# Moving S5 and the convolution within a mixer, and regrouping three products of RWKV

## The chip, the cores and the metric

One NeuronCore of one Trainium2 chip runs the whole kernel in one launch. The metric is the device time in microseconds; three runs of the kernel before gave 1250.41, 1250.13 and 1246.07 us, so the median is 1250.13. The engines are TensorE (PE, with its weight loads as PEld), VectorE (DVE), ScalarE (ACT), GpSimd (POOL) and SyncE (SP, which issues most transfers).

## The reference, cut to what matters

The program is a trunk of two layers on 256 positions of width 1024, float32. Each layer adds half a SwiGLU, then a mixer, then half a second SwiGLU; a last norm ends it. The mixer projects the normalised input and lets four branches work on it side by side:

```
for l in range(DEPTH):
    x = x + 0.5 * swiglu(rmsnorm(x, ffn1_norm[l]), ...)
    h = rmsnorm(x, mix_norm[l]);  p = h @ w_in[l]
    u_a, u_b, r_p, k_p, v_p, z_in, b_g, c_g, gate_pre = split(p)
    y_a = s5_mixer(u_a, ...)                # diagonal complex state space, 16 groups
    y_b = pool_mixer(u_b, ...)              # trailing means
    y_c = rwkv7_mixer(h, r_p, k_p, v_p, ...)  # delta rule, decay per channel, 4 heads
    y_d = b_g * causal_conv3(c_g * z_in)    # short convolution
    merged = sum over the four of (y_b @ w_branch[l, b]) * sigmoid(gate_b)
    x = x + merged @ w_out[l]
    x = x + 0.5 * swiglu(rmsnorm(x, ffn2_norm[l]), ...)
```

RWKV's recurrence is computed in chunks of 64 positions: for every chunk and head a matrix of pairs is formed (the products of keys, gates and receptances with their decays), a triangular matrix of it is inverted, and the states are carried from chunk to chunk.

## The kernel before, in words

**Weights.** All large products go through units: a unit is a 256x512 block of a weight matrix. SyncE loads it (raw), ScalarE rounds it to the high part (wh, L253), VectorE forms the residue (wl = raw - wh, L225 through `finish`), and TensorE takes three matmuls for each 128 rows: high by high (L259), high by low weight (L260), low by high (L261). Four units have room at a time. The high part of a unit is issued six steps before its first matmul, its residue five steps before.

**Order of the work.** The order on every engine is fixed at build time by the class `Flow`. The main thread is a list of steps; in a mixer one step is two ticks, and a tick is three matmuls of 512 columns. The branches are generator threads that yield waits: `wA(n)` means "go on at the start of the n-th next step", `wT(n)` "after n ticks", and `wM(n, b)` "after n ticks, when b PSUM banks are free, and only one such thread in a tick", the first in the list (RWKV, convolution, S5, pool). These numbers decide only where instructions stand in the queue of their engine; at run time every engine works through its queue in order, and an instruction waits for its inputs alone.

**The steps of a mixer**, counted from 0 at the low-rank columns: 0 to 39 the projections (low-rank; r and k; ua and ub; v and z; bg and cg), 40 to 55 the gates of the pool branch, 56 to 59 that branch's product (Y[1]), 60 to 75 the gates of the convolution branch, 76 to 79 its product, then S5's (96 to 99) and RWKV's.

**RWKV (L909 to L1325).** At steps 36 to 40 VectorE forms the decays, bvec and kp, rk (L1033), the planes of W and BK; GpSimd forms DG (L1030, the diagonal with a chunk's last decay), copies the values v into two planes of W (L1053), and forms the two halves of KB (L1054, L1055, keys times the decay to the chunk's end). At ticks 90 and 94 follow the pair matrices Gm (matmuls L1073), which read BK and three planes of W. GpSimd then takes small diagonal blocks of them (dg, L1084, sixteen copies), forms the levels Bl and Rd, and four rounds of inversion run from tick 116 on (L1102): each is a matmul on Bl and Tm, a copy Xm on ScalarE, a matmul on Rd and Xm, and Tm = p + Tm on VectorE, three ticks apart. The values in W and KB are first read by the transposes L1123 and L1124 (tick 100), DG by MT (L1236).

**S5 (L1328 to L1436).** us goes to memory and comes back as U8 (L1342). `wM(38, 1)` (L1344) counts from there to the matmuls sT; from sT follow, in fixed distances, sN, the transposes sS, the copies sX, six VectorE operations (gA, gB, gt), two scans (L1378), two GpSimd products, Hs (L1385), the matmuls sY (L1392), the gelu and the glu product. The steps are such that sT stands at tick 98.

**Convolution (L1480 to L1508).** zc = cg * zin at step 44; `wA(14)` (L1496) puts the taps (cv, L1499 and L1501) at steps 58 and 59, the product with bg at 60 and the split into high and low at 61.

Of the kernel before, what the change touches and what calls it, by code (L numbers as in the profile page):

```python
# [11 lines left out]
AF = mybir.ActivationFunctionType  # L12
# [12 lines left out]
C = 64  # L25
# [25 lines left out]
def wA(n=1):  # L51

    return ("A", n, 0)
# [17 lines left out]
def wM(n=1, banks=0):  # L71

    return ("M", n, banks)
# [98 lines left out]
def trunk_kernel(ctx: ExitStack, tc: tile.TileContext, a, out, dbg=None):  # L172
    nc = tc.nc
    ve, sc, gp, pe = nc.vector, nc.scalar, nc.gpsimd, nc.tensor
# [19 lines left out]
    def cc(name):  # L194
        o, n = CONST_COLS[name]
        return cst[:, o:o + n]
# [11 lines left out]
    def bank(name="pb"):  # L208
        assert fl.banks > 0
        fl.banks -= 1  # L210
        return pp.tile([128, 512], F32, name=name, tag="pb")

    def free(n=1):
        fl.banks += n
        assert fl.banks <= NB
# [8 lines left out]
    def tt(o, i0, i1, op=ALU.mult, eng=ve):  # L224
        eng.tensor_tensor(out=o, in0=i0, in1=i1, op=op)  # L225
# [292 lines left out]
    def col(l, name, i=0):  # L518
        r, n = vrow[name]
        return vec[:, r + l * n + i:r + l * n + i + 1]  # L520
# [277 lines left out]
    def mixer(l):  # L798
# [3 lines left out]
        def et(shape, nm, dt=F32):  # L802
            return st["mp"].tile(shape, dt, name=nm, tag="e", bufs=NE)

        def ft(shape, nm):
            return st["mp"].tile(shape, F32, name=nm, tag="f", bufs=NF)

        def e2(nm):
            return et([128, 2, S], nm)

        def enter():
            st["mp"] = es_.enter_context(tc.tile_pool(name=f"mix{l}", bufs=1))
            spawn(rwkv())
            spawn(conv())
            spawn(s5())
            spawn(pool())
# [76 lines left out]
        def until(name):  # L893
            while name not in got:
                yield wA(1)
# [3 lines left out]
        def ysplit(b, src):  # L899
            h, lo = et([128, 2, S], f"yh{b}", F32R), et([128, 2, S], f"yl{b}", F32R)  # L900
            split(h, lo, src)
            Y[b] = (h, lo)

        def dump(nm, src):
            if dbg is not None and l == 0:
                sp.dma_start(out=dbg[nm].rearrange("(j p) t -> p j t", p=128), in_=src)


        def rwkv():  # L909
# [9 lines left out]
            def tshift(ps, i, nm):  # L919
                z = e2(nm)  # L920
                for j in range(2):
                    sc.activation(z[:, j], ps[:, j], AF.Copy, scale=om[:, 2 * i + j:2 * i + j + 1])
                for j in range(2):
                    ve.scalar_tensor_tensor(out=z[:, j, 1:], in0=ps[:, j, :S - 1],
                                            scalar=col(l, "rwkv_mu_rkv", 2 * i + j),
                                            in1=z[:, j, 1:], op0=ALU.mult, op1=ALU.add)
                return z
# [76 lines left out]
            v_ = tshift(got["v"], 2, "v")  # L1004
# [16 lines left out]
            Pt, Pm, iP, PC = L0[:, 0], L0[:, 1], L1[:, 0], L1[:, 1]  # L1021
            bvec, kp = e2("bvec"), e2("kp")
# [4 lines left out]
            yield wA(1)  # L1027
            DG = et([128, 8, C], "DG")
            id8 = cc("id64").unsqueeze(1).to_broadcast([128, 8, C])
            tt(DG, id8, Pt[:, :, C - 1:C].to_broadcast([128, 8, C]), eng=gp)  # L1030
            rk = e2("rk")
            for j in range(2):
                ve.scalar_tensor_tensor(out=rk[:, j], in0=r_[:, j], scalar=col(l, "rwkv_r_k", j), in1=kp[:, j],  # L1033
# [3 lines left out]
            W = st["mp"].tile([128, 4, 6, C], F32, name="W")  # L1037
            KB2 = ft([128, 4, 4, C], "KB2")
            BK = ft([128, 4, 4, C], "BK")

            def me(t_):
                return t_.rearrange("p j (m e t) -> p (j m) e t", m=2, e=2)

            def mf(t_):
                return t_.rearrange("p (q e) t -> p q e t", e=2)
# [4 lines left out]
            tt(W[:, :, 2::3], me(r_), mf(Pt))  # L1050
            yield wA(1)
            tt(BK[:, :, 1:3], me(kp), mf(iP))
            gp.tensor_copy(W[:, :, 1::2][:, :, 0:2], me(v_))  # L1053
            tt(KB2[:, :, 0::3], me(bvec), mf(PC), eng=gp)  # L1054
            tt(KB2[:, :, 1:3], me(kp), mf(PC), eng=gp)  # L1055

            def small_tile(nm):
                return st["mp"].tile([128, 8, 32], F32, name=nm, tag="q", bufs=7)
# [5 lines left out]
            for j in range(2):  # L1064
                yield wM(10 if j == 0 else 4, 2)
                ps = [bank("gm").rearrange("p (c t) -> p c t", c=4) for _ in range(2)]
                for c in range(4):
                    m, o = c // 2, c % 2
                    for e in range(2):
                        es = slice(64 * e, 64 * e + 64)  # L1070
                        lhs = BK[es, 2 * j + m, 2 * o:2 * o + 2].rearrange("p k t -> p (k t)")
                        rhs = W[es, 2 * j + m, 0:3:2] if o == 0 else W[es, 2 * j + m, 4:6]
                        pe.matmul(ps[e][:, c], lhsT=lhs, rhs=rhs, start=True, stop=True)  # L1073
                yield wA(1)
                for e in range(2):
                    h = 2 * j + e
                    g_ = et([128, 4, 128], f"Gm{h}")
                    tt(g_, ps[e], maskb)
                    free()
                    Gm.append(g_)  # L1080
                    gv = g_.rearrange("p (m o) s -> p o m s", o=2)
                    for q in range(4):
                        qs, cs = slice(32 * q, 32 * q + 32), slice(32 * (q % 2), 32 * (q % 2) + 32)
                        gp.tensor_copy(dg[qs, 2 * h:2 * h + 2], gv[qs, q // 2, :, cs])  # L1084
# [157 lines left out]
            for c in range(3):  # L1242
                for h in range(4):
                    j, e = h // 2, h % 2
# [14 lines left out]
            for c in range(1, 3):  # L1259
                yield wM(2 if c > 1 else 4, 1)  # L1260
                p = bank("zc").rearrange("p (j s) -> p j s", s=C)
                for h in range(4):
                    j, e = h // 2, h % 2
# [64 lines left out]
        def s5():  # L1328
# [12 lines left out]
            U8 = et([128, G, 32], "U8")  # L1341
            sp.dma_start(out=U8, in_=ud.rearrange("g h i b -> (h i) g b"))  # L1342

            yield wM(38, 1)  # L1344
            sT = bank("sT").rearrange("p (u s) -> p u s", u=4)
            for u in range(4):
                for q in range(4):
# [132 lines left out]
        def conv():  # L1480
            yield from until("z_in")
            yield wA(1)
            zin = e2("zin")
            sc.activation(zin, got["z_in"], AF.Copy)
            free()
            yield from until("bg")
            yield wA(1)
            bg = e2("bg")
            sc.activation(bg, got["bg"], AF.Copy)
            free()  # L1490
            yield from until("cg")
            yield wA(1)
            zc = e2("zc")
            tt(zc, got["cg"], zin)
            free()
            yield wA(14)  # L1496
            cv = e2("cv")
            for j in range(2):
                sc.activation(cv[:, j], zc[:, j], AF.Copy, scale=col(l, "conv_w", 4 + j))  # L1499
                for w in (1, 0):  # L1500
                    ve.scalar_tensor_tensor(out=cv[:, j, 2 - w:], in0=zc[:, j, :S - 2 + w],  # L1501
                                            scalar=col(l, "conv_w", 2 * w + j), in1=cv[:, j, 2 - w:],
                                            op0=ALU.mult, op1=ALU.add)
                yield wA(1)
            tt(cv, cv, bg)
            yield wA(1)
            ysplit(3, cv)
            dump("yd", cv)  # L1508
# [185 lines left out]
```

## Time and profile before

| | |
|---|---|
| median of three runs | 1250.13 us (1246.07 to 1250.41) |
| profiled execution | 1247.8 us, span 1246.0 us |
| mean granted TensorE clock | 0.997 |
| TensorE busy | 1224.4 us, 98% |
| VectorE, ScalarE, GpSimd busy | 761.9, 616.8, 372.8 us |

Busy shares are means over the whole span. The mixers lie at about 208 to 410 us and 822 to 1024 us; the other stretches are the feed-forward halves. A wait of an engine is listed with what ended it; where the time of an instruction includes waiting for a shared resource, the instruction shows as longer.

### The profile page before, as it was taken

What the parts mean: (1) busy time and instruction counts of PE and PEld (TensorE: products, weight loads), DVE (VectorE), ACT (ScalarE), POOL (GpSimd) and SP (SyncE); (2) the same over time, 40 slices, a digit from 0 to 9 for tenths busy, and PEclk for the clock granted to TensorE, in tenths of its full rate; (3) what the DMA queues carried; (4) which work ended last, traced back from release to release, by engine and by line L of the source; (5) the groups of instructions that cost most, each with busy time, mean ns of one, the idle gap of its engine ahead of it and who ended that gap; (6) DMA issues with size and microseconds to landing.
All of it is one profiled execution on the core that took longest, in us unless ns stands there. A gap on an engine that the chain in (4) does not pass through costs nothing.

```text
span 1246.0 us, 18893 instructions
## 1 busy us (share of the span) xinstructions
PE 1224.4 (98%) x7280; PEld 1000.1 (80%) x7280; DVE 761.9 (61%) x943; ACT 616.8 (50%) x787; POOL 372.8 (30%) x504
## 2 busy tenths in 40 slices
PE   8999999999999999999999999999999999999997
PEld 6888878887778888888888887888777788888885
DVE  6955656488566665554465555474885667555543
ACT  6454435665444464444364444366654445544433
POOL 4694394054132000000069454313512220000001
PEclk9999999999999999999999999999999999999999
DMA  8676555554446566655676565566443556666561
GB/s 255 182 220 182 182 177 165 179 148 139 123 133 196 176 185 186 186 181 191 187 200 179 177 193 179 158 189 181 152 122 105 158 187 193 188 186 186 185 191 63
DMA packets 139922, 216.28 MB, mean 174 GB/s; under 512 B 30348, under 2 KB 42488, under 8 KB 139832
## 3 DMA queue, kind: packets, MB, share of 16 engines
q1 hardware_dynamic: 138552, 213.63, 56.8%
q10 hardware_dynamic: 1120, 1.40, 0.3%
q8 instruction: 57, 0.93, 0.3%
q0 software_dynamic: 160, 0.05, 0.1%
q14 instruction: 33, 0.27, 0.1%
HBM read 212.29 MB, written 1.57 MB: 172 GB/s over the span
## 4 chain that ended last, share of the span: by engine, by line
PE 93%; DVE 5%; issue 1%; ACT 0%; DMA 0%; POOLq 0%; SPq 0%; POOL 0%; DVEq 0%; ACTq 0%
PE acc L259 29%; PE acc L260 28%; PE acc L261 28%; PE pb L271 3%; DVE wl L225 1%; PE inv L1102 1%; DVE cv L1501 0%; PE pb L778 0%; DVE rk L1033 0%; PE gm L1073 0%; DMA vr<-in_ffn_norm_dram 0%; PE lr L953 0%; PE wu L1207 0%; PE sY L1392 0%; DVE mg L225 0%
## 5 line engine op out<-in xcount | busy, mean ns | idle before, releaser
L225 DVE TENSOR_TENSOR wl<-raw,wh 128x1024 fp32r<-128x1024 f32 (+1 forms) x398 | 506.7, 1274 | 293.9 <-ACT wh L253 287.8
L253 ACT ACTIVATE wh<-raw 128x1024 fp32r<-128x1024 f32 (+1 forms) x393 | 415.0, 1056 | 416.9 <-PE acc L261 399.4
L259 PE MATMUL acc<-wh,xh 128*128 128x512 f32 x1152 | 462.0, 401 | 0.0
L260 PE MATMUL acc<-wl,xh 128*128 128x512 f32 x1152 | 450.2, 391 | 1.0 <-DVE wl L225 0.8
L261 PE MATMUL acc<-wh,xl 128*128 128x512 f32 x1152 | 450.3, 391 | 0.0
L259 PEld LDWEIGHTS acc<-wh,xh 128*128 128x128 f32 x1152 | 216.9, 188 | 47.7 <-issue 4.5
L261 PEld LDWEIGHTS acc<-wh,xl 128*128 128x128 f32 x1152 | 216.8, 188 | 46.4
L260 PEld LDWEIGHTS acc<-wl,xh 128*128 128x128 f32 x1152 | 217.1, 188 | 44.6 <-DVE wl L225 2.3
L259 PE MATMUL acc<-wh,hh 128*128 128x512 f32 x352 | 139.4, 396 | 0.0
L261 PE MATMUL acc<-wh,hl 128*128 128x512 f32 x352 | 137.6, 391 | 0.0
L260 PE MATMUL acc<-wl,hh 128*128 128x512 f32 x352 | 137.3, 390 | 0.0
L225 POOL TENSOR_TENSOR wl<-raw,wh 128x1024 fp32r<-128x1024 f32 x3 | 7.2, 2385 | 255.8 <-ACT wh L253 255.8
L261 PEld LDWEIGHTS acc<-wh,hl 128*128 128x128 f32 x352 | 66.1, 188 | 15.3
L259 PEld LDWEIGHTS acc<-wh,hh 128*128 128x128 f32 x352 | 66.1, 188 | 14.9 <-issue 1.3
L260 PEld LDWEIGHTS acc<-wl,hh 128*128 128x128 f32 x352 | 66.1, 188 | 13.9
L431 DVE SCALAR_TENSOR_TENSOR hd<-acc,rs,sg 128x512 f32<-128x512 f32 (+1 forms) x48 | 33.7, 703 | 33.3 <-PE acc L261 29.9
L336 POOL TENSOR_SCALAR pre<-ss 128x1 f32<-128x1 f32 x2 | 0.4, 224 | 171.4 <-ACT junk L284 171.4
L225 POOL TENSOR_TENSOR mg<-mg,gate 128x512 f32<-128x512 f32 x16 | 29.6, 1867 | 67.2 <-DVE gate L225 67.2
L222 DVE TENSOR_TENSOR hl<-pb,hh 128x512 fp32r<-128x512 f32 (+1 forms) x48 | 28.8, 642 | 32.3 <-ACT hh L221 32.2
L221 ACT ACTIVATE hh<-pb 128x512 fp32r<-128x512 f32 (+1 forms) x48 | 24.4, 561 | 42.2 <-PE pb L271 42.2
L424 ACT ACTIVATE sg<-acc,rs 128x512 f32<-128x512 f32 (+1 forms) x48 | 31.1, 654 | 20.6 <-PE acc L261 18.8
L794 POOL COPY LK<-LKt 128x512 f32<-128x512 f32 x8 | 11.0, 1403 | 66.1 <-DMA LKt<-kp 66.1
(349 smaller groups left out, 1149.0 us busy)
## 6 DMA issues: line engine op xcount, KB each, us to landing
raw<-in_w_in_dram SPq DMA_DIRECT2D x96, 512.0 KB
raw<-in_ffn_w_down_dram SPq DMA_DIRECT2D x88, 512.0 KB
raw<-in_ffn_w_up_dram SPq DMA_DIRECT2D x80, 512.0 KB
raw<-in_ffn_w_gate_dram SPq DMA_DIRECT2D x79, 512.0 KB
raw<-in_w_branch_dram SPq DMA_DIRECT2D x16, 512.0 KB
raw<-in_w_out_dram SPq DMA_DIRECT2D x16, 512.0 KB
raw<-in_ffn_w_gate_dram SPq DMA_DIRECT2D x18, 256.0 KB
raw<-in_ffn_w_up_dram SPq DMA_DIRECT2D x16, 256.0 KB
```

The costliest lines, as they stand in the source:

```text
L221: sc.activation(dh, src, AF.Copy)
L222: eng.tensor_tensor(out=dl, in0=src, in1=dh.bitcast(F32), op=ALU.subtract)
L225: eng.tensor_tensor(out=o, in0=i0, in1=i1, op=op)
L253: sc.activation(self.h, self.r, AF.Copy)
L259: pe.matmul(ps, lhsT=lh, rhs=wh, start=first, stop=False)
L260: pe.matmul(ps, lhsT=lh, rhs=wl, start=False, stop=False)
L261: pe.matmul(ps, lhsT=ll, rhs=wh, start=False, stop=last)
L271: pe.transpose(b[:, j * 128:(j + 1) * 128], src[:, j * 128:(j + 1) * 128], ident)
L424: sc.activation(sg[:, :n], pg[:, :n], AF.Silu, scale=rstd[t])
L431: ve.scalar_tensor_tensor(out=hd[:, :n], in0=pu, scalar=rstd[t], in1=sg[:, :n], op0=ALU.mult, op1=ALU.mult)
L794: gp.tensor_copy(LK[:, 4 * (q - 1 + h_):4 * (q + h_)], LKt[:, 4 * h_:4 * h_ + 4].rearrange("p g i h -> p g h i"))
L1102: pe.matmul(p[qs, u], lhsT=lhs[qs, u], rhs=rhs[qs, u], start=True, stop=True)
```

## The change

1. DG (L1030) is formed behind the second pair matrices, in the loop over j, instead of before rk.
2. Both halves of KB (L1054, L1055) are formed behind the first pair matrices.
3. The values are copied into W by ScalarE instead of GpSimd (L1053).
4. S5's sT comes 28 ticks behind the load of U8 instead of 38 (L1344).
5. The taps of the convolution come 22 steps behind zc instead of 14 (L1496).

All matmuls, transfers and operands stay as they are.

```
             DG = et([128, 8, C], "DG")
             id8 = cc("id64").unsqueeze(1).to_broadcast([128, 8, C])
-            tt(DG, id8, Pt[:, :, C - 1:C].to_broadcast([128, 8, C]), eng=gp)
             rk = e2("rk")
...
             tt(BK[:, :, 1:3], me(kp), mf(iP))
-            gp.tensor_copy(W[:, :, 1::2][:, :, 0:2], me(v_))
-            tt(KB2[:, :, 0::3], me(bvec), mf(PC), eng=gp)
-            tt(KB2[:, :, 1:3], me(kp), mf(PC), eng=gp)
+            sc.activation(W[:, :, 1::2][:, :, 0:2], me(v_), AF.Copy)
...
                         pe.matmul(ps[e][:, c], lhsT=lhs, rhs=rhs, start=True, stop=True)
                 yield wA(1)
+                if j == 0:
+                    tt(KB2[:, :, 0::3], me(bvec), mf(PC), eng=gp)
+                    tt(KB2[:, :, 1:3], me(kp), mf(PC), eng=gp)
+                else:
+                    tt(DG, id8, Pt[:, :, C - 1:C].to_broadcast([128, 8, C]), eng=gp)
                 for e in range(2):
...
-            yield wM(38, 1)
+            yield wM(28, 1)
             sT = bank("sT").rearrange("p (u s) -> p u s", u=4)
...
-            yield wA(14)
+            yield wA(22)
             cv = e2("cv")
```

## Rows read from the trace of the kernel before

**Rows 1.** The page: busy us by engine, and the chain that ended last.
```profile
PE 1224.4 (98%) x7280; PEld 1000.1 (80%) x7280; DVE 761.9 (61%) x943; ACT 616.8 (50%) x787; POOL 372.8 (30%) x504
...
PE 93%; DVE 5%; issue 1%; ACT 0%; DMA 0%; POOLq 0%; SPq 0%; POOL 0%; DVEq 0%; ACTq 0%
```
**Rows 2.** Waits of TensorE, whole span: us in total, times, longest.
```profile
PE inv L1102 <- DVE Tm L225: 5.0, 2, 2.5
PE inv L1102 <- issue: 1.0, 1, 1.0
PE acc L260 <- DVE wl L225: 0.8, 2, 0.4
PE inv L1102 <- DVE Tm L1137: 0.5, 2, 0.2
```
**Rows 3.** Timeline of TensorE, layer 0: start, us, instruction [idle before].
```profile
284.70 1.08 PE L1349 MATMUL sT<-LS,U 128*32 128x128 f32 x32
...
306.54 0.40 PE L259 MATMUL acc<-wh,xh 128*128 128x512 f32 x1
...
307.24 0.39 PE L259 MATMUL acc<-wh,xh 128*128 128x512 f32 x1
...
310.58 0.82 PE L1102 MATMUL inv<-Tm,Bl 32*32 32x32 f32 x64 [2.50 <-DVE Tm L225]
...
312.82 0.40 PE L259 MATMUL acc<-wh,xh 128*128 128x512 f32 x1
```
**Rows 4.** Timeline of TensorE, layer 1.
```profile
924.06 1.08 PE L1102 MATMUL inv<-Tm,Bl 32*32 32x32 f32 x64 [2.50 <-DVE Tm L225]
...
927.63 0.39 PE L259 MATMUL acc<-wh,xh 128*128 128x512 f32 x1
```
**Rows 5.** Stretch of layer 1: us; busy PE, PEld, DVE, ACT, POOL; clock; DMA share, GB/s.
```profile
926.00:927.00 1.00, 1.00 (x4) 0.72 (x3) 1.00 (x2) 0.00 (x0) 0.00 (x0) 0.50 0.65 250
```
**Rows 6.** Timeline of VectorE, layer 0, RWKV's products.
```profile
266.87 2.08 DVE L225 TENSOR_TENSOR wl<-raw,wh 128x1024 fp32r<-128x1024 f32 x1
268.88 2.27 DVE L1033 SCALAR_TENSOR_TENSOR rk<-r,vec,kp 128x256 f32<-128x256 f32 x2
...
273.98 1.21 DVE L225 TENSOR_TENSOR wl<-raw,wh 128x1024 fp32r<-128x1024 f32 x1
```
**Rows 7.** Timeline of GpSimd, layer 0, the same stretch.
```profile
266.40 1.48 POOL L225 TENSOR_TENSOR DG<-cst,L 128x512 f32<-128x512 f32 x1 [4.84 <-ACT L L1019]
267.82 1.61 POOL L1053 COPY W<-v 128x512 f32<-128x512 f32 x1
269.39 1.48 POOL L225 TENSOR_TENSOR KB<-bvec,L 128x512 f32<-128x512 f32 x1
```
**Rows 8.** Timeline of VectorE, layer 0, ahead of the long wait.
```profile
300.40 1.22 DVE L1378 TENSOR_TENSOR_SCAN gA<-R,gA 128x512 f32<-128x512 f32 x1
...
303.98 2.29 DVE L1501 SCALAR_TENSOR_TENSOR cv<-zc,vec,cv 128x255 f32<-128x255 f32 x2
...
306.80 0.99 DVE L1501 SCALAR_TENSOR_TENSOR cv<-zc,vec,cv 128x255 f32<-128x255 f32 x2
307.70 0.67 DVE L225 TENSOR_TENSOR Hs<-gA,gB 128x496 f32<-128x496 f32 x1
...
308.89 1.22 DVE L225 TENSOR_TENSOR wl<-raw,wh 128x1024 fp32r<-128x1024 f32 x1
```
**Rows 9.** Stretches of layer 0, columns as in rows 5.
```profile
260.00:280.00 20.00, 19.58 (x103) 15.74 (x102) 19.81 (x24) 12.63 (x18) 7.46 (x7) 1.00 0.41 122
...
284.00:292.00 8.00, 8.00 (x73) 6.48 (x72) 3.52 (x5) 4.51 (x9) 4.95 (x12) 1.00 0.55 171
292.00:311.00 19.00, 16.25 (x259) 12.66 (x258) 18.62 (x27) 9.86 (x15) 5.09 (x4) 1.00 0.37 111
319.00:332.00 13.00, 13.00 (x317) 9.79 (x315) 8.24 (x13) 7.01 (x12) 1.44 (x2) 1.00 0.39 124
```
**Rows 10.** Timeline of ScalarE, layer 0: the copy of bg.
```profile
271.94 0.60 ACT L1489 ACTIVATE bg<-bg 128x512 f32<-128x512 f32 x1
```

## The prediction

> **What bounds the kernel now.** I read the page's busy times first, then its chain, then the waits of TensorE, then the timelines around the longest of these waits. TensorE is busy for 1224.4 of 1246.0 us and carries 93% of the chain that ended last [rows 1]; no other engine passes 61%. So the time is TensorE's work plus its holes, and a change that leaves every matmul in place, as this one does, can only move the holes. The waits of TensorE [rows 2] list those that lie within the two mixers: 5.0 us in two waits of an inversion matmul (L1102) for VectorE's Tm, 1.0 us in one L1102 gap with no releaser, 0.8 us in two waits of L260 for a weight residue wl, and 0.5 us in two waits for Tm's first transpose. Together 7.3 us; every one but the 1.0 us comes once per layer.
>
> The timeline shows why the long one exists [rows 3]: the inversion matmul ought to follow the group at 307.24 at once, at about 308.0, and starts at 310.58. On VectorE the queue in front of Tm is then [rows 8]: two convolution taps at 303.98 (2.29 us for the pair; the second pair takes 0.99), the second pair at 306.80, Hs of S5 at 307.70, a residue wl at 308.89. VectorE works in order, so Tm's addition waits behind all of them. The stages [rows 9] show the same on a larger scale: VectorE is busy 19.81 of 20 us at 260 to 280, only 3.52 of 8 us at 284 to 292, then 18.62 of 19 us at 292 to 311, and 8.24 of 13 us at 319 to 332. There are two valleys, and the work of S5 and of the convolution both lie on the ridge between them.
>
> In layer 1 the wait is followed by something more. The stretch 926 to 927 shows a granted clock of 0.50 [rows 5], the lower level of 1.2 GHz, after 2.5 us in which TensorE did nothing. From the inversion matmul to the sixth matmul after it take 927.63 - 924.06 = 3.57 us [rows 4], against 312.82 - 310.58 = 2.24 us in layer 0 [rows 3] at full clock: 1.33 us more.
>
> **The change part by part.** One group of three matmuls is a tick, 307.24 - 306.54 = 0.70 us [rows 3]; a step of the mixer is two ticks, 1.4 us.
>
> *S5 sooner.* 38 to 28 ticks puts the sT matmuls ten ticks (7 us) ahead of their 284.70 [rows 3], between two groups at about 274.4. Everything in S5 that counts from there moves five steps: the copies sN and sX on ScalarE, six multiplications and additions, two scans and Hs on VectorE, two multiplications on GpSimd, then sY, the gelu and the glu matmuls. No transfer moves: the load of U8 is issued where it was. The six operations have the shape of Hs, some 0.67 us each, of which 0.6 before the next one starts, and a scan takes 1.22 [rows 8], so this is 7 x 0.6 + 2 x 1.2 = 6.6 us in all. It goes from the ridge at 292 to 311 into the valley at 284 to 292, which has 8 - 3.52 = 4.5 us free [rows 9]. It does not all fit; about 2 us spill past 292. That matters little, because a residue wl is issued five steps (some 7 us) before TensorE needs it, so VectorE may be 5 us late before TensorE feels it. The sT matmuls themselves come just ahead of the place where TensorE now waits 0.4 us for wl [rows 2] and fill it. Cost of the new place: if U8 were not there at 274, TensorE would stand up to 7 us per layer; sT shows no idle time ahead of it now [rows 3] and its load is issued 24 ticks or more ahead of the new place too, so I take 0 and keep 7 as the far end.
>
> *Convolution later.* 14 to 22 steps moves four taps, one multiplication and one residue (2.29 + 0.99, and two of Hs's size, 1.3 us [rows 8]) and three ScalarE copies from steps 58 to 61 to steps 66 to 69, in the later valley (319 to 332, less what the holes give back), where VectorE has 13 - 8.24 = 4.8 us free, and S5 has left its gelu too. Its result is first read at step 76, so no branch waits. Here Tm of the third and fourth inversion round is behind it: a round leaves three ticks (2.1 us) between the matmul whose sum Tm takes and the next reader, and the queue ahead of Tm is at most one wl (1.21 us [rows 6]) and one multiplication. I take 0 to 0.3 us for that.
>
> *KB behind the pair matrices.* The two KB multiplications are issued after the first pair matrices, but they need only bvec, kp and PC, and GpSimd has nothing queued ahead of them any more. Issue order is no gate between engines: the copy of the values is issued two steps after rk and yet ran at 267.82 [rows 7], ahead of rk at 268.88 [rows 6]. So KB will start at about 267, two microseconds sooner than now, not at 279. There it holds VectorE up as now: wl at 266.87 took 2.08 us against 1.21 at 273.98, rk at 268.88 took 2.27 [rows 6] against 0.99 for a like pair [rows 8], while GpSimd multiplied [rows 7]. What goes away is DG's share, 2.08 - 1.21 = 0.9 us; KB's 2.27 - 0.99 = 1.3 us on rk stay, whatever it costs the next multiplication as well.
>
> *DG among the dg copies.* It is 1.48 us of GpSimd [rows 7] put between two runs of eight small copies, so Rd comes about 1.5 us later plus what the copies slip. Its reader, Tm's first transpose, is issued twenty ticks (14 us) after the second pair matrices; cost 0, at most 1.5 us per layer if that cover went. It falls upon VectorE's pair products; between 0 and 1.48 us of VectorE time, I take 0.5, in a stretch with slack.
>
> *Values on ScalarE.* One activation of 128x512, about 0.60 us like the copy of bg [rows 10], ahead of yh and the weight copies in a stretch where ScalarE is busy 12.63 of 20 us [rows 9]. GpSimd loses 1.61 us. A weight copy is 0.6 us late there, inside the 5 us slack. Cost 0, at most 0.6 per layer.
>
> **Sum.** Removed: 7.3 us of waits and 1.33 us of low clock. Of the 1.0 us without a releaser I count half, as nothing in the change addresses it. New waits 0.3. So 7.3 - 0.5 + 1.33 - 0.3 = 7.8 us. The profiled execution took 1247.8 us (span 1246.0 and 1.8 around it): 1247.8 - 7.8 = 1240.0. The median of the runs shown is 2.3 us above it, which would make 1242.3. I say 1241.
>
> Of the clock: layer 0 shows the same 2.5 us idle with no drop, so the price in another execution is 0 to 2.7 us for both layers. The Trainium skill (TensorE: Matmul & The Clock Gate, Part 1) says that the low level is the default and that sustained activity lifts it, with two levels only. The 0.50 of [rows 5] agrees. By the rule, without the idle time there is no drop, and all of 1.33 is won; by layer 0's row alone the drop is chance and the sum would be 6.5.
>
> **The rivals.** *The hole moves* (1244 to 1246). S5 now follows directly on RWKV's busy stretch, so VectorE gets no rest from 260 to about 296; if it is then over 5 us late, L260 waits for wl near 290 to 297. For it: 19.81 of 20 us busy, and 2 us that do not fit. Against it: at 284 to 292 VectorE now has 4.5 us free, so whatever it was late at 280 is made good there before the spill of 2 us begins. Price: half of the 7.8 is given back, 1247.8 - 3.9 = 1243.9, or 1246 from the median.
>
> *Nothing comes of it* (1248 to 1250). The long wait stays because the order of weights and Tm on VectorE, not the extra work, makes it. Against it: rounds two to four, with as much wl and less else, show no wait [rows 2].
>
> *Slower* (1254). The convolution stands at steps 66 to 69 in front of Tm of rounds three and four. If VectorE reaches step 66 some 5 us late, as now at step 58, both rounds wait 2.5 us and the clock may fall each time: per layer 2 x (2.5 + 1.33) = 7.7, two layers 15.3; 1247.8 - 8.6 + 15.3 = 1254.5. It decides from a lateness of about 1 us at Tm. Against it: 4.8 us are free there and S5's tail has moved ahead.
>
> **How the numbers follow.** Forecast 0.64, the hole moves 0.20, nothing 0.08, slower 0.08. About 0.5% is what a measurement of this kernel tells from no change; against 1250.13 that is 1243.9. Of the forecast nine tenths lie below it (0.58), of the second a fifth (0.04): faster 0.62. The rest of these and the third make no change 0.30, the last slower 0.08. The range: low end all waits, both drops of the clock and the lowest run, about 1237; high end the second case from the median and a little of the third, 1247.
>
> **What would show it.** TensorE's waits of VectorE's Tm gone in both layers, no stretch at 0.50 clock near the inversion; sT between two groups near 274; VectorE's share even from 284 to 311; KB still near 267 on GpSimd and rk still over 2 us; cv at steps 66 to 69. I am wrong if L260 waits for wl by more than 1 us, if an inversion round waits for Tm in a later place, or if sT waits for U8.

## The result, and the profile after

The changed kernel took 1241.01 us (median; 1240.82 to 1241.55) against 1248.61 us (the median of four runs, one more than above), a ratio of 0.9939 (0.9925 to 0.9952): 7.6 us or 0.6% faster. The profiled execution took 1241.55 us with a span of 1239.7, which is 6.3 us less than the span of the kernel before. Below are the page's busy times and chain, and then TensorE's waits. In the chain, VectorE's 5% [rows 1] have become 0%.

```profile
PE 1222.7 (99%) x7280; PEld 999.5 (81%) x7280; DVE 759.2 (61%) x943; ACT 616.9 (50%) x789; POOL 369.8 (30%) x502
...
PE 98%; issue 0%; DMA 0%; DVE 0%; ACT 0%; SPq 0%; POOLq 0%; POOL 0%; DVEq 0%; ACTq 0%
```
```profile
PE pb L508 <- DMA vr<-in_ffn_norm_dram: 5.1, 1, 5.1
PE inv L1104 <- DVE Tm L1139: 1.9, 2, 1.0
PE pb L271 <- DMA x<-in_x_dram: 1.6, 1, 1.6
PE inv L1104 <- issue: 0.4, 1, 0.4
```

The waits for Tm's addition (5.0 us) and for wl (0.8 us) [rows 2] are gone. One has grown: the wait for Tm's first transpose (now L1139) from 0.5 to 1.9 us, 0.96 per layer. Within the mixers 7.3 us have become 2.3; with the 1.33 us of low clock that makes 6.3, and the spans differ by as much. To the tenth this is chance: the two DMA waits at the kernel's start grew from 6.0 to 6.7 us, and smaller differences make up for it. Around the inversion of layer 1 the granted clock is now 1.00 (columns as in [rows 5]):

```profile
902.00:924.00 22.00, 21.04 (x404) 16.30 (x405) 17.09 (x24) 13.17 (x21) 6.04 (x5) 1.00 0.48 146
```

The timeline of TensorE in layer 0 shows sT in its new place, the grown wait, and the second inversion round at 310.73, for which TensorE stood 2.50 us before [rows 3] and which now follows at once:

```profile
275.12 1.08 PE L1351 MATMUL sT<-LS,U 128*32 128x128 f32 x32
...
302.71 0.74 PE L1104 MATMUL inv<-Tm,Bl 32*32 32x32 f32 x64 [0.96 <-DVE Tm L1139]
...
310.73 0.75 PE L1104 MATMUL inv<-Tm,Bl 32*32 32x32 f32 x64
```

The stretches of [rows 9], with the same columns:

```profile
260.00:280.00 20.00, 20.00 (x132) 16.11 (x131) 18.86 (x24) 13.57 (x20) 5.92 (x6) 1.00 0.43 132
...
284.00:292.00 8.00, 8.00 (x46) 6.74 (x44) 7.90 (x10) 2.79 (x4) 5.89 (x12) 1.00 0.29 92
292.00:311.00 19.00, 18.04 (x313) 13.98 (x311) 14.83 (x22) 11.29 (x18) 5.38 (x4) 1.00 0.50 146
...
319.00:332.00 13.00, 13.00 (x267) 10.09 (x267) 8.66 (x16) 6.28 (x10) 2.88 (x4) 1.00 0.37 121
```

VectorE's valley is filled (3.52 to 7.90 of 8 us), its ridge cut (18.62 to 14.83 of 19 us). VectorE around RWKV's products, and GpSimd beside it:

```profile
267.44 1.22 DVE L225 TENSOR_TENSOR wl<-raw,wh 128x1024 fp32r<-128x1024 f32 x1
268.58 2.96 DVE L1032 SCALAR_TENSOR_TENSOR rk<-r,vec,kp 128x256 f32<-128x256 f32 x2
```
```profile
267.67 2.15 POOL L225 TENSOR_TENSOR KB<-bvec,L 128x512 f32<-128x512 f32 x1 [5.54 <-DVE bvec L1026]
269.77 1.48 POOL L225 TENSOR_TENSOR KB<-kp,L 128x512 f32<-128x512 f32 x1
```

KB starts as soon as bvec is there, 1.7 us sooner than before [rows 7], and not behind the pair matrices; wl gets ahead of it (1.22 us, was 2.08) and rk waits longer (2.96, was 2.27) [rows 6].

### The profile page after: what moved, and what is told of

It is laid out like the page before. It is cut to its first block, busy times and chain, and to the rows that moved or that the text cites. A ratio compares the mean times of both kernels' runs of the same rounds, so it can differ in the third digit from the quotient of the medians.

```text
span 1239.7 us, 18891 instructions
## 1 busy us (share of the span) xinstructions
PE 1222.7 (99%) x7280; PEld 999.5 (81%) x7280; DVE 759.2 (61%) x943; ACT 616.9 (50%) x789; POOL 369.8 (30%) x502
## 4 chain that ended last, share of the span: by engine, by line
PE 98%; issue 0%; DMA 0%; DVE 0%; ACT 0%; SPq 0%; POOLq 0%; POOL 0%; DVEq 0%; ACTq 0%
PE acc L259 30%; PE acc L261 29%; PE acc L260 29%; PE pb L271 3%; PE inv L1104 1%; DMA x<-in_x_dram 0%; PE pb L778 0%; PE gm L1070 0%; PE lr L953 0%; PE wu L1209 0%; PE sY L1394 0%; PE pb L774 0%; PE glu L1425 0%; DVE wl L225 0%; PE po L1253 0%
## 5 line engine op out<-in xcount | busy, mean ns | idle before, releaser
L260 PE MATMUL acc<-wl,xh 128*128 128x512 f32 x1152 | 449.6, 390 | 0.1
L260 PEld LDWEIGHTS acc<-wl,xh 128*128 128x128 f32 x1152 | 216.8, 188 | 43.0 <-DVE wl L225 0.6
L260 PE MATMUL acc<-wl,hh 128*128 128x512 f32 x352 | 137.3, 390 | 0.0
L260 PEld LDWEIGHTS acc<-wl,hh 128*128 128x128 f32 x352 | 66.1, 188 | 13.9
```

Source lines behind the costliest of these rows:

```text
L260: pe.matmul(ps, lhsT=lh, rhs=wl, start=False, stop=False)
```

## The experiments

Ratios are to the kernel before, run beside each version on the same chip.

**S5 alone.**
```
-            yield wM(38, 1)
+            yield wM(28, 1)
```


> S5 ten ticks sooner and nothing else. Ridge theory (VectorE has too much queued from 292 to 311; any 3 us taken off ends the long wait for Tm): S5 takes 6.6 us off, the 2.5 us wait per layer falls below 0.5, the wl wait of 0.4 goes because sT fills it, the wait for Tm's first transpose grows to about 1 us as in the changed kernel; 1242 to 1243.5 against 1248.6. Taps theory (only the convolution's taps issued ahead of Tm make the wait): at least 1.5 us of it stays per layer; 1245 to 1247.

1239.97 us, ratio 0.9932 (0.9918 to 0.9947). TensorE's waits in the mixers and VectorE's queue in front of Tm's addition:

```profile
PE inv L1102 <- DVE Tm L1137: 1.9, 2, 1.0
...
PE inv L1102 <- issue: 0.3, 1, 0.3
```
```profile
303.52 1.39 DVE L1501 SCALAR_TENSOR_TENSOR cv<-zc,vec,cv 128x255 f32<-128x255 f32 x2
...
305.43 0.99 DVE L1501 SCALAR_TENSOR_TENSOR cv<-zc,vec,cv 128x255 f32<-128x255 f32 x2
...
306.96 1.22 DVE L225 TENSOR_TENSOR wl<-raw,wh 128x1024 fp32r<-128x1024 f32 x1
308.10 0.42 DVE L225 TENSOR_TENSOR Tm<-inv,Tm 128x256 f32<-128x256 f32 x1
```

The taps still stand in front of Tm, and Tm is in time all the same: the taps theory is refuted. The whole gain of the change is here, the new wait too. But the time also lies below the 1242 to 1243.5 of the ridge theory, and the theory's measure (6.6 us off the ridge) does not show at Tm. Rows of VectorE, GpSimd and TensorE in layer 0, first of the kernel before, then with S5 moved:

```profile
301.54 0.42 DVE L1137 STREAM_TRANSPOSE Tm<-Rd 128x256 f32<-128x256 f32 x1
...
302.45 1.60 DVE L225 TENSOR_TENSOR wl<-raw,wh 128x1024 fp32r<-128x1024 f32 x1
...
302.93 2.28 POOL L225 TENSOR_TENSOR gB<-gB,TS 128x512 f32<-128x512 f32 x1
...
310.02 0.42 DVE L225 TENSOR_TENSOR Tm<-inv,Tm 128x256 f32<-128x256 f32 x1
...
317.12 0.43 PE L1392 MATMUL sY<-LK,U 128*32 128x128 f32 x8
```
```profile
301.32 0.43 DVE L1137 STREAM_TRANSPOSE Tm<-Rd 128x256 f32<-128x256 f32 x1
...
302.39 1.22 DVE L225 TENSOR_TENSOR wl<-raw,wh 128x1024 fp32r<-128x1024 f32 x1
...
303.46 0.43 PE L1392 MATMUL sY<-LK,U 128*32 128x128 f32 x8
...
309.91 0.75 PE L1102 MATMUL inv<-Tm,Bl 32*32 32x32 f32 x64
```

Tm's first transpose, which stands ahead of the wait, comes no sooner than before (301.32 and 301.54). From there two things close the hole. VectorE reaches Tm's addition 1.9 us sooner (308.10 for 310.02): Hs is gone from the queue (0.6 us), and a residue (1.22 for 1.60) and the first taps (1.39 for 2.29) are quicker now that S5's two products no longer run on GpSimd beside them. And TensorE wants Tm 1.9 us later (309.91 for about 308.0 [rows 3]), because S5's own matmuls sY, at 317 before, now stand at 303.46 to 305.35, ahead of the second round. Which of the two matters more no run separates, and none moved GpSimd's products alone.

**Convolution alone.**
```
-            yield wA(14)
+            yield wA(22)
```


> Convolution eight steps later and nothing else. Ridge theory: 4.6 us come off VectorE ahead of Tm, the 2.5 us wait per layer goes and with it the low clock; the wl wait (0.4 per layer) and the wait for the first transpose (0.24) stay; 1242 to 1243. Taps theory: the same, 1242 to 1243. Were S5 the cause instead, 1247 or more.

1242.89 us, 0.9952 (0.994 to 0.9965). Tm's addition still makes TensorE wait, but only half a microsecond per layer, and a gap without a releaser appears:

```profile
PE inv L1102 <- issue: 1.6, 1, 1.6
...
PE inv L1102 <- DVE Tm L225: 1.0, 2, 0.5
PE acc L260 <- DVE wl L225: 0.8, 2, 0.4
PE inv L1102 <- DVE Tm L1137: 0.5, 2, 0.2
```

Here sY stays where it was and Tm's addition comes 2.2 us sooner (307.82), though 3.3 us of taps are gone: Hs, still in front of it, now stands for GpSimd.

```profile
305.06 1.10 DVE L225 TENSOR_TENSOR Hs<-gA,gB 128x496 f32<-128x496 f32 x1 [0.59 <-POOL gB L225]
...
307.82 0.41 DVE L225 TENSOR_TENSOR Tm<-inv,Tm 128x256 f32<-128x256 f32 x1
```

Either move shortens what stands in front of Tm enough or nearly so. That is the ridge theory as far as it goes; S5's move does somewhat more, and sY's new place is part of it.

**Both moves, without the regrouping** (the two edits above together).

> Both moves, with DG, KB and the values formed as before on GpSimd. My sum gives the regrouping at most 0.8 us (the wl wait that sT fills anyway): 1241 to 1242, within 1 us of the changed kernel. If the regrouping matters (3 us of VectorE freed near 270), 1243 or more, with waits of L260 for wl.

1240.81 us, 0.9938 (0.9926 to 0.9951), the changed kernel's ratio; its only wait in the mixers is the 1.9 us for Tm's first transpose. So the moves do not add up, and the regrouping gives nothing.

**The regrouping alone** (the changed kernel with 38 and 14).

> Regrouping of DG, KB and the values alone; S5 and convolution as before. Mine: the wl wait (0.8 in both layers) falls to 0.3 or less as VectorE is 0.6 to 0.9 us less late there, the long wait stays at 2.0 to 2.5 per layer: 1247 to 1248.5, no difference that can be measured. Rival: VectorE's lateness carries over from 270 to 310 and the long wait shrinks by the same 0.9 us: 1246. Slower rival: DG among the dg copies makes Rd late: the wait for the first transpose grows by 1 us per layer, 1250.

1247.72 us, 0.9997 (0.9988 to 1.0006): no difference. The wl wait is gone, as expected, and the long one is whole, so lateness at 270 does not carry over to 310:

```profile
PE inv L1104 <- DVE Tm L225: 5.1, 2, 2.5
...
PE inv L1104 <- DVE Tm L1139: 0.5, 2, 0.2
```

**What makes the new wait.** VectorE in the changed kernel: a residue idles for ScalarE, then Hs, another residue, then the transpose. ScalarE itself had stood 6.2 us:

```profile
299.12 1.37 DVE L225 TENSOR_TENSOR wl<-raw,wh 128x1024 fp32r<-128x1024 f32 x1 [1.86 <-ACT wh L253]
300.41 0.66 DVE L225 TENSOR_TENSOR Hs<-gA,gB 128x496 f32<-128x496 f32 x1
301.00 1.21 DVE L225 TENSOR_TENSOR wl<-raw,wh 128x1024 fp32r<-128x1024 f32 x1
302.13 0.43 DVE L1139 STREAM_TRANSPOSE Tm<-Rd 128x256 f32<-128x256 f32 x1
```
```profile
293.01 0.38 ACT L1132 ACTIVATE UV<-tmA 64x256 f32<-64x256 f32 x1 [6.20 <-DVE RH L1131]
```

**UV first.**
```
-                ve.tensor_copy(RH[0:64, hs, :, 0], pr_[0:64, 0])
-                ve.tensor_copy(RH[64:128, hs, :, 0], pr_[64:128, 1])
                 sc.activation(UVv[64:128, 0, hs], pr_[64:128, 0], AF.Copy)
                 sc.activation(UVv[0:64, 1, hs], pr_[0:64, 1], AF.Copy)
+                ve.tensor_copy(RH[0:64, hs, :, 0], pr_[0:64, 0])
+                ve.tensor_copy(RH[64:128, hs, :, 0], pr_[64:128, 1])
```


> Changed kernel, but ScalarE's two copies into UV are issued ahead of VectorE's two copies into RH, which read the same PSUM bank. The new 0.96 us wait per layer for Tm's first transpose: theory through ScalarE (ScalarE stands 6.2 us behind VectorE's late RH, so the next weight copies and then the residues in front of Tm come late): ScalarE's idle time before UV falls under 1 us, the wait falls from 0.96 to under 0.3, 1239.2 to 1239.8. Rival (VectorE itself is that late, ScalarE only waits along): the wait stays over 0.7, 1241.

1241.59 us, 0.9944 (0.9929 to 0.9958): my theory missed, and the rival's figures held. ScalarE is free (UV at 288.58, 1.77 us idle), the residue runs at 297.29, and VectorE stands still all the same, now in Hs, for GpSimd's gB. The wait is 0.80 us:

```profile
297.29 1.33 DVE L225 TENSOR_TENSOR wl<-raw,wh 128x1024 fp32r<-128x1024 f32 x1
299.80 1.11 DVE L225 TENSOR_TENSOR Hs<-gA,gB 128x496 f32<-128x496 f32 x1 [1.18 <-POOL gB L225]
...
301.97 0.43 DVE L1139 STREAM_TRANSPOSE Tm<-Rd 128x256 f32<-128x256 f32 x1
```

**Hs later**, in the changed kernel and with UV first:
```
-            yield wA(3)
+            yield wA(6)
             tt(Hs[:, :, 1:32], gA[:, :, 0:31], gB[:, :, 0:31], ALU.subtract)
-            yield wM(9, 1)
+            yield wM(3, 1)
```


> Changed kernel, but Hs is issued on VectorE three steps later, behind Tm's first transpose; sY stays at its tick. In the changed kernel Hs and a residue stand between a residue that waits for ScalarE (to 299.1) and Tm. Hs theory alone (VectorE stands in Hs for GpSimd's gB): the wait of 0.96 us falls to 0 to 0.1, 1239.2. Two paths, each hidden behind the other (ScalarE late behind RH; Hs behind gB): ScalarE's weight copies are still late, so 0.4 to 0.7 us of the wait is left, 1240 to 1240.5.

1240.58 us, 0.9938 (0.9917 to 0.9959); the wait is 0.53 us per layer, as the two paths gave.

> UV first on ScalarE and Hs three steps later together. Two paths: with both out of the way Tm's transpose is done near 301 and the wait is 0 to 0.2 us, 1239.2, as with the transpose moved. If a third thing holds VectorE (residues late by themselves, or the place of Hs costs sY): 0.5 us or more is left or turns up at sY, 1240 or more.

1239.93 us, 0.9933 (0.9916 to 0.9951); no wait for Tm is left in either layer. So two paths led to the wait, each hidden behind the other: through ScalarE behind RH, and through Hs behind GpSimd. Taking one away gave 0.15 or 0.4 us of 0.96, both together all of it.

**Tm's transpose early**, ahead of both.
```
+            ve.transpose(out=flat(Tm), in_=flat(Rd))
             yield wM(8, 2)
-            ve.transpose(out=flat(Tm), in_=flat(Rd))
```


> Changed kernel, but Tm's first transpose is issued on VectorE behind the BKt copies (step 53) instead of ahead of the akv matmuls (tick 114). Both theories of the 0.96 us wait: it goes, since Rd is there at 290.4 and the transpose no longer stands behind two residues and Hs; 1.9 us in both layers, 1239.1. If another instruction of the first inversion round is late as well (Bl, Hs for sY), less comes of it: 1240.5 and a wait at that place.

1239.35 us (1238.36 to 1239.69), 0.9928 (0.9912 to 0.9943), against 1241.59 (1239.95 to 1242.22) of UV first, run beside it: no wait for Tm is left, and TensorE has no wait over 0.5 us in the mixers.

**KB kept back** (both KB products issued behind the first eight dg copies).
```
                 for e in range(2):
...
+                if j == 0:
+                    tt(KB2[:, :, 0::3], me(bvec), mf(PC), eng=gp)
+                    tt(KB2[:, :, 1:3], me(kp), mf(PC), eng=gp)
```


> Changed kernel, but both KB products are issued behind the first eight dg copies, so that GpSimd's own order keeps them until the first pair matrices are there (near 283 instead of 267.7). Mine: rk falls from 2.96 to about 0.9 us and VectorE is 2 us less late at 272, where TensorE does not wait: no gain there. KB then meets S5's two-SBUF products at 284 to 290 and pushes Rd and S5's chain back by 2 to 3 us: the wait for Tm's first transpose grows from 0.96 to 2 or 3 us per layer, 1243 to 1245. Rival (freeing the stretch at 268 is what counts): 1240 or less.

1242.56 us, 0.9959 (0.9946 to 0.9973), below the 1243 to 1245 expected. In the trace the wait grew as expected, though by less: 1.6 us per layer instead of 0.96. The times alone do not show a loss, as the interval overlaps that of the changed kernel; the profiled execution, with a drop of the clock in layer 0, was the longest of eight (1245.86). rk took 0.88 us and nothing was gained by it. VectorE beside KB (GpSimd 284.12 to 286.7) and DG (286.63 to 287.7):

```profile
284.68 1.29 DVE L225 TENSOR_TENSOR Gm<-gm,cst 128x512 f32<-128x512 f32 x2 [2.10 <-PE gm L1070]
285.88 0.68 DVE L225 TENSOR_TENSOR gA<-sS,TC 128x512 f32<-128x512 f32 x1
...
287.08 1.70 DVE L225 TENSOR_TENSOR wl<-raw,wh 128x1024 fp32r<-128x1024 f32 x1
```

The products with one input in PSUM (gm, sS) take no longer than elsewhere; wl, with two inputs in SBUF, takes 1.70 us for 1.2. The Trainium skill (GPSIMD Engine Reference, section 8, Key points) names two SBUF inputs as one of two cases in which a VectorE instruction contends with GpSimd; these rows agree.

**S5 alone with UV first and Tm early**, convolution and GpSimd as before.

> Kernel before with S5 ten ticks sooner, UV copies first and Tm's first transpose early; convolution and DG, KB, values as before. If the S5 move carries all of the gain and the 0.96 us wait is the only thing that it costs: no wait of TensorE over 0.5 us in the mixers, 1238 to 1238.6, ahead of the changed kernel by 2.5. If the convolution's place matters once the rest is gone (taps ahead of Tm at step 58): a wait of 0.5 us or more at Tm's addition per layer, 1239 to 1240.

1239.25 us (1238.56 to 1239.96), 0.9928 (0.9914 to 0.9942); no wait of Tm or wl, one gap without a releaser of 0.9 us. The taps in their old place cost nothing, but the time missed the 1238 to 1238.6 that I expected. This and the version with Tm's transpose early have the lowest ratio, the same in both. The changed kernel was not run beside them, and the ratios' intervals overlap; the missing 1.9 us of waits speak for them. Their spans (1237.3 and 1237.4 against 1239.7) do so less: S5 alone, with the same 1.9 us of waits, has 1238.4. So a gain over the changed kernel is likely and not shown by times.

## Why the prediction was right

- *TensorE's holes are all that can move*: right. With what was measured the sum is 7.3 - 0.4 + 1.33 - 1.9 = 6.3 us instead of 7.8, and the span fell by 6.3.
- *S5 into the valley*: the step that carries the result, but in part by a way that the prediction did not have. With S5 moved alone, only Hs of the 6.6 us of VectorE work, 0.6 us, came out from in front of Tm's addition. The rest of the gain there was, by the rows, the end of a meeting with GpSimd (the taps' 2.29 us had been taken as their own cost, and a like pair takes 0.99), and TensorE's hole was also filled by sY, which the prediction lists as moving and gives no worth. VectorE's share did not become even: 99% at 284 to 292 and 78% at 292 to 311. sT came at 275.12 (274.4 said; the prediction's 7 us ahead of 284.70 would be 277.7, and it was 9.6, as two groups of pair matrices and the wait for wl stand between), U8 was there, and L260 waits for no wl. The rival of the moved hole had it right that VectorE would be full well past 292; it still was not late enough for wl.
- *New waits 0.3 us*: mis-sized. It was 1.9 us, at Tm's first transpose, a place that I had costed at nothing for DG's sake and not looked at for S5's. Hs and a residue now stand in front of it. The runs showed both paths.
- *The 1.0 us gap*: counted half, 0.4 left, so the size was right. That nothing in the change addresses it was not: in the three kernels with S5 in its old place it lies in layer 0 (1.0, 1.6 and 1.0 us), in those with S5 sooner it lies in layer 1 (0.3 to 0.9 us), and with both moves alone there is none. It goes with S5's place; what it is stays open.
- *Convolution later, at 0 to 0.3 us*: no cost. It also gave nothing beside S5's move, though 5.3 us alone. I had counted one sum for both moves and not seen that either is nearly enough.
- *KB at 267, DG's share the only gain, values on ScalarE free*: right; the regrouping alone is 0.9997. KB's price on rk was mis-sized, 2.1 us (2.96 against 0.88 with KB kept back) and not 1.3.
- *1241 between the profiled execution and the median*: that 1241.01 was met so closely is luck. The sum was 1.5 us too high against the profiled execution, and 1241 was set between two starting points. The profiled execution fell by 6.3, the median by 7.6. The runs of the kernel before spread over more than 4 us, the changed kernel's four lie within 0.7 us. The mean granted clock on record for each execution goes with this: of 35 executions of the kernel before, beside the experiments, the 20 with 0.997 or 0.998 took 1246.08 to 1248.60 us and the 15 with 0.995 or 0.996 took 1248.14 to 1251.69; the changed kernel's four all have 0.998. That fits a median that gains more than the profiled execution, which had one drop of the clock, in layer 1. Where the drops lie in the unprofiled executions was not seen.

## What to carry to other kernels

Where the bound engine's holes come from another engine's queue, draw that engine's busy share by stretches, and move one whole chain from a ridge into a valley; a second move out of the same ridge gains little. Then count at the place of the hole itself: what left the queue in front of the late instruction, what there was slow only beside another engine, and what work the bound engine gets to do just ahead of the hole. Count at every later reader what now stands in front of it in the queue: a wait that was 0.24 us became 0.96 because the moved chain ended just there. And an instruction's place in the code is only a place in one queue: what is to run late must be put behind something that is late.

## What the runs showed of the hardware

The granted clock fell to 0.50 (1.2 GHz) after a wait of 1.61 us in layer 0 of the kernel with KB kept back,

```profile
306.00:308.00 2.00, 2.00 (x34) 1.55 (x36) 0.91 (x2) 0.22 (x1) 0.81 (x1) 0.50 0.75 250
```

and stayed at 1.00 after 1.59 us in layer 1 of the same execution and after 2.50 us in layer 0 of the kernel before, while in its layer 1 it fell after 2.50 us [rows 5]. In these rows the length of one hole does not tell whether the clock falls; the price is to be taken as a chance. Where it fell it was 1.33 us before and 1.6 us here (from the inversion matmul to the first group behind sY 304.60 to 309.65 in layer 0, 916.71 to 920.17 in layer 1).
